# Block sums for adaLN, a two-product group norm, and a fixed four-engine order for the convolution stage

## The chip, the cores and the metric

One core of a Trainium2 chip runs the kernel. The metric is device time in microseconds (us) of one execution. "Before" is the kernel as it stood, "after" the changed one. PE is TensorE, DVE is VectorE, ACT is ScalarE, POOL is GpSimd, and SP is the engine whose queue issues most DMAs.

## The reference

A trunk of two layers runs over 512 tokens of width 1024. Layer 0 mixes tokens with a short gated convolution, layer 1 with a Mamba-2 state-space mixer (SSD). A SwiGLU FFN follows each. Around every sub-layer stand RMS norms and adaLN: the vector c gives a shift, a scale and a gate for each sub-layer.

```
mod = (silu(c) @ ada_w + ada_b).reshape(bsz, DEPTH, 2, 3, D_MODEL)
h = rmsnorm(x, norm_g[i, 0]) * (1.0 + scale) + shift
b_gate, c_gate, v = split(h @ w_in, 3);  y = (b_gate * causal_conv(c_gate * v, conv_w)) @ w_out      # layer 0
y = ssd(...) * silu(z);  y = rms_normalize(y in 8 groups of 256) * norm_g;  y = y @ w_out            # layer 1
x = x + gate * rmsnorm(y, norm_g[i, 1])
y = (silu(gate) * up) @ w_out with gate, up = split(h @ w_in, 2)                                     # FFN
```

All of it is float32.

## The kernel before

**Matmuls.** A weight and its operand are each split into a high part (rounded to fp32r) and a low remainder; three fp32r products (high x high, high x low, low x high: `mm3`, L261 to L264) replace one float32 product. One chunk (`in_chunk`) makes 128 output columns for all 512 tokens with 8 x 3 matmuls. `load_w` (L205) brings two chunks of weights (1 MB) by one DMA on SP into a staging tile `wst`, of which there are two; ACT casts the high part (L202) and DVE subtracts for the low part (L203), into one of four `whl` tiles. `load_wo` (L226) does the same for output matrices, and `load_lead` (L240) for the first weights of the next sub-layer, which go into tiles of their own.

**adaLN.** `ada_set` (L130) handles 512 columns of `ada_w`: four DMAs of 512 KB, and eight multiply-adds on DVE (L124, L126) into `ada_acc`, so that each partition holds the partial sum of its own rows. `ada_finish` (L115) sums over the partitions: four PE transposes of 128x128, then a reduce on DVE (L120). `ada_fin` adds the bias and makes scales and gate columns. There are 20 such sets behind the opening: `ada_next` starts six in the convolution stage and 14 in the first FFN, and finishes each set one call later. `put_gates` turns gate columns into rows and writes them to memory; `make_gg` reads them back as a broadcast tile.

**Convolution stage.** An opening in an order written out by hand (`OPENING`) makes h and the first six chunks (`li`, b, c and v of channels 0 and 1). Then the loop over `jp` makes c and v chunks for two channel blocks, gates them (c copied by ACT, v times c on DVE, the middle tap on ACT, two taps on DVE, then b times that on DVE, high part on ACT, low part on DVE), and six more adaLN sets run beside it. This loop is not in a hand order: a scheduler places each engine's instructions by priority and its own costs. The output product follows in `out_begin` and `out_finish`: half 0 of the columns (`pieces(0)`: k 0 to 3, then 4 and 5), the second half (`pieces(1)`: k 0 to 3), and the rest of k in the boundary, whose order (`BOUNDARY`) is written out: it squares, norms, updates x, transposes, and begins the next sub-layer's six lead chunks. The lead weights of the FFN are loaded in `finish`, behind all loads of the output matrix.

**SSD stage.** Eight groups run in a hand order on PE, ACT and DVE. For each, ACT squares two tiles, DVE adds them (`accg`, L1133), and one float32 matmul with a matrix of ones (`ssg`, L1144) sums over partitions; the root and the scaling follow in the next group's step.

Of the kernel before, what the change touches and what calls it, by code (L numbers as in the profile page):

```python
# [35 lines left out]
def trunk_kernel(  # L36
# [33 lines left out]
    pool.memset(ones, 1.0)  # L70
    mask = consts.tile([P, P], F32, name="mask")
# [7 lines left out]
    csil = consts.tile([P, KD], F32, name="csil")  # L79
# [14 lines left out]
    def other_vectors(stage):  # L94
        d_rows = stage[:16, 3, :].rearrange("p (a b) -> p a b", b=HD)
        d16 = stage[:16, 4, 0:2]
        dma_s(stage[0:16, 0, :], m_norm_g.rearrange("i (r p) -> (i r) p", p=P))
        dma_s(stage[:32, 1, :], m_conv_b.rearrange("i (r p) -> (i r) p", p=P))
        dma_s(stage[:, 2, :], m_conv_w.rearrange("i k (r p) -> (i k r) p", p=P))
        dma_s(d16, m_d.rearrange("i (r p) -> (i r) p", p=2))  # L100
        turned(stage[:, 0, :], mng, 16)
        turned(stage[:, 1, :], mcb, 32)
        turned(stage[:, 2, :], cols3, P)
        dve.tensor_copy(d_rows, d16.unsqueeze(2).to_broadcast([16, 2, HD]))
        turned(d_rows.rearrange("p a b -> p (a b)"), dcol, 16)

# [7 lines left out]

    def ada_finish(acc, ncol, dst):  # L115
        n = ncol // P
        pt = aux_ps("ada_ps")
        for b in range(n):
            pe.transpose(pt[:, b * P:(b + 1) * P], acc[:, b * P:(b + 1) * P], ident)
        dve.tensor_reduce(dst, pt[:, :ncol].rearrange("p (a b) -> p a b", b=P), axis=AX.X, op=ADD)  # L120
# [18 lines left out]
    def ada_fin(col0, acc):  # L139
        q = col0 // P  # L140
        ada_finish(acc, 512, mods[:, q:q + 4])
        dve.tensor_add(mods[:, q:q + 4], mods[:, q:q + 4], adab[:, q:q + 4])
        s, r = divmod(q, 24)
        kind, j = divmod(r, 8)
        if kind == 1:
            dve.scalar_tensor_tensor(acol[:, s * 8 + j:s * 8 + j + 4], mods[:, q:q + 4], 1.0,
                                     ncol(s, 0, j, 4), ADD, MUL)
        elif kind == 2:
            dve.tensor_mul(gcol[:, s * 8 + j:s * 8 + j + 4], mods[:, q:q + 4], ncol(s, 1, j, 4))
# [143 lines left out]
    def put_gates(s):  # L293

        pt = aux_ps("ggp")
        pe.transpose(pt[:KD, :P], gcol[:, s * KD:(s + 1) * KD], ident)
        gr = tmp.tile([KD, P], F32, tag="gr", name="gr", bufs=1)
        dve.tensor_copy(gr, pt[:KD, :P])
        dma(gate_d[s], gr)

# [250 lines left out]
    ada_open = []  # L551

    def ada_next(n):
        for _ in range(max(n, 1)):
            if ada_open:
                ada_fin(*ada_open.pop())
            if ada_sets and n:
                c0 = ada_sets.pop(0)
                ada_open.append((c0, ada_set(c0)))
# [4 lines left out]
    with ExitStack() as ph:  # L564
        ada_p.append(ph.enter_context(tc.tile_pool(name="adap", bufs=3, reuse_waits="tile")))
        actp = ph.enter_context(tc.tile_pool(name="actp", bufs=22, reuse_waits="tile"))
        gx = ph.enter_context(tc.tile_pool(name="gx", bufs=1, reuse_waits="tile"))

# [87 lines left out]
        def busy(dst, n):  # L656

            for _ in range(n):
                pe.matmul(dst, ident, ident, start=True, stop=True)

        with tc.manual_schedule(engines={PE_ENGINE, mybir.EngineType.SP, mybir.EngineType.Activation,
# [121 lines left out]

            for name in OPENING.split():
                step(name)
            later = []
            next_cv = [load_w([(w_in0, (i + 1) * D + 2 * P, 256)], later=later) for i in range(2)]
            for hi, lo in later:
                hi()
                lo()  # L790


        def conv_mix_cv(jc, psc, psv):
            cs = t2("c_sb")
            act.copy(cs, psc)
            cv = t2("cv")
            dve.tensor_mul(cv, psv, cs)
            u = t2("u_cv")
            act.activation(u, cv, AF.Copy, scale=acw[:, 16 + jc:17 + jc])
            dve.scalar_tensor_tensor(u[:, 1:], cv[:, :T - 1], acw[:, 8 + jc:9 + jc], u[:, 1:], MUL, ADD)  # L800
            dve.scalar_tensor_tensor(u[:, 2:], cv[:, :T - 2], acw[:, jc:jc + 1], u[:, 2:], MUL, ADD)
            return u

        def conv_mix_b(u, psb, a):
            dve.tensor_mul(u, psb, u)
            act.copy(a[:, 0, :], u)
            dve.tensor_tensor(a[:, 1, :], u, a[:, 0, :].bitcast(F32), SUB)

        acts = []
        for jp in range(0, KD, 2):  # L810
            if jp == 0:
                pss = lead_ps[:4]
            else:
                ws = next_cv[0] + next_cv[1] if jp == 2 else [
                    w for i in range(2) for w in load_w([(w_in0, (i + 1) * D + jp * P, 256)])]
                pss = [in_chunk(w, h) for w in ws]
            us = [conv_mix_cv(jp + b, pss[b], pss[2 + b]) for b in range(2)]
            wb = load_w([(w_in0, jp * P, 256)]) if jp else None
            for b in range(2):
                a = act_tile(f"bu{jp + b}")  # L820
                conv_mix_b(us[b], in_chunk(wb[b], h) if jp else lead_ps[4 + b], a)
                acts.append(a)
            ada_next(2 if jp < 6 else 0)
            if jp == 4:
                put_gates(0)
                gg = make_gg(0, gg_tile)
                other_vectors(actp.tile([P, 8, P], F32, tag="a", name="rows2"))
        def ffn_lead(i, tile4):
            w1 = f_w_in[i]
            return lambda: [w for c0 in (0, DFF, 256) for w in load_lead([(w1, c0, 256)], tile4)]  # L830

        def ffn_after(i):
            return lambda: load_w([(f_w_in[i], DFF + 256, 256)])

        begun = out_finish(out_begin(0, w_out0, lambda k: acts[k], KD, [gg], xn_tile, "aux",
                                     ffn_lead(0, tile4), ffn_after(0)))


        def ffn(s, i, begun, act_tile, gg_tile, xn_tile, ada, gates, lead, after):
# [13 lines left out]
            for f in range(0, NF, 2):  # L853
# [12 lines left out]
                if f == 18:  # L866
                    for q in gates:
                        put_gates(q)
                    gg = make_gg(s, gg_tile)
# [12 lines left out]
        assert not ada_sets and not ada_open  # L882


    with ExitStack() as ph:
# [99 lines left out]
        class Group:  # L985
# [120 lines left out]
            def step_c(self, q):  # L1106
# [20 lines left out]
                if q == 0:  # L1127
                    self.accg = t2("accg")
                    act.activation(self.accg, y0, AF.Square)
                else:  # L1130
                    sqg = t2("sqg")
                    act.activation(sqg, y0, AF.Square)
                    dve.tensor_add(self.accg, self.accg, sqg)  # L1133
                ygs.append(y0)

            def step_d(self):
                self.sums()
                self.root()
                self.norm()

            def sums(self):

                self.ssg = aux_ps("ssg")
                pe.matmul(self.ssg, ones, self.accg, start=True, stop=True)  # L1144
# [37 lines left out]
        with tc.manual_schedule(engines={PE_ENGINE, mybir.EngineType.Activation, mybir.EngineType.DVE}):  # L1182
# [69 lines left out]
            next(conv2[2])  # L1252
            next(conv2[3])
# [7 lines left out]
            for g in range(1, NG - 1):  # L1261
# [41 lines left out]
                next(conv2[3])  # L1303
                nxt.project_z(0)
# [83 lines left out]
```

## Time and profile before

| | us |
|---|---|
| time, median of 3 runs (lowest, highest) | 1380.81 (1379.1, 1381.97) |
| the profiled execution's own time | 1383.75 |
| its span, first to last instruction | 1382.0 |
| PE busy | 1366.8 |
| DVE busy | 841.6 |
| ACT busy | 535.4 |
| POOL busy | 1.5 |
| mean granted clock of PE | 0.998 of full speed |

Lines of the profile read: line of the code, engine, operation, what it writes <- what it reads, shapes, count | busy time, mean ns of one | idle time of the engine just before, and what ended it. In a timeline the first two figures are start and duration. In a row of windows stand the window, its length, the busy time of PE, PEld (weight loads, beside PE), DVE, ACT and POOL with counts, then PE's granted clock, the DMA engines' busy share and GB/s. A float32 matmul leaves two records.

### The profile page before, as it was taken

Reading aid. Unit: us, or ns where it says so; the run is one execution under the profiler, and the core shown is the slowest. Engines: PE = TensorE matmul, PEld = TensorE weight load, DVE = VectorE, ACT = ScalarE, POOL = GpSimd, SP = SyncE. Lnnn points to the kernel's source line nnn. Section 1 sums busy time; section 2 is a strip of 40 time slices with the busy share of each in tenths; the row PEclk is TensorE's granted clock in tenths of the full one; section 3 lists DMA queues with packets and bytes.
Section 4 is the critical chain, followed back from the end, with each engine's and each line's share of the span. In section 5 each row is a group of like instructions: output and inputs, shape, how many; then the busy total and the mean of one; then the engine's idle time right before and its main releaser. Section 6 shows DMA issues by size and latency. Waiting matters only on the chain.

```text
span 1382.0 us, 17400 instructions
## 1 busy us (share of the span) xinstructions
PE 1366.8 (99%) x7035; PEld 1147.2 (83%) x7035; DVE 841.6 (61%) x1331; ACT 535.4 (39%) x817; POOL 1.5 (0%) x11
## 2 busy tenths in 40 slices
PE   8999999999999999999999999999999999999998
PEld 7788879888888888898888888888888888888886
DVE  5887756487775222759988898897573333332224
ACT  5432256222222211745555445564472322222112
POOL 0000000000000000000000000000000000000000
PEclk9999999999999999999999999999999999999999
DMA  9966661368773223415343423313403223322221
GB/s 313 328 205 230 211 211 62 122 213 268 237 257 122 92 92 102 116 47 172 107 138 109 136 84 115 128 57 121 154 30 107 92 93 113 99 92 92 92 92 62
DMA packets 154181, 190.36 MB, mean 138 GB/s; under 512 B 5860, under 2 KB 111220, under 8 KB 153076
## 3 DMA queue, kind: packets, MB, share of 16 engines
q1 hardware_dynamic: 149952, 176.34, 39.8%
q10 hardware_dynamic: 4148, 12.90, 2.9%
q8 instruction: 55, 0.90, 0.3%
q14 instruction: 26, 0.21, 0.1%
HBM read 186.98 MB, written 2.24 MB: 137 GB/s over the span
## 4 chain that ended last, share of the span: by engine, by line
PE 65%; DMA 1%; DVE 1%; ACT 1%; issue 0%; DVEq 0%; ACTq 0%
PE ip L262 11%; PE ip L264 11%; PE ip L263 11%; PE y L362 7%; PE y L364 7%; PE y L363 7%; PE li L262 2%; PE li L264 2%; PE li L263 2%; PE yd L1118 1%; DMA wst<-in_f_w_in_dram 1%; PE yo L1112 1%; PE xtr L478 1%; PE cb L1057 1%; PE xtok L1040 1%; PE st L1073 0%
## 5 line engine op out<-in xcount | busy, mean ns | idle before, releaser
L262 PE MATMUL ip<-h,whl 128*128 128x512 f32 x1096 | 433.2, 395 | 0.0
L264 PE MATMUL ip<-h,whl 128*128 128x512 f32 x1096 | 427.2, 390 | 0.0
L263 PE MATMUL ip<-h,whl 128*128 128x512 f32 x1096 | 426.8, 389 | 0.0
L262 PEld LDWEIGHTS ip<-h,whl 128*128 128x128 f32 x1096 | 205.8, 188 | 44.1 <-issue 2.6
L263 PEld LDWEIGHTS ip<-h,whl 128*128 128x128 f32 x1096 | 205.9, 188 | 43.2 <-issue 1.4
L264 PEld LDWEIGHTS ip<-h,whl 128*128 128x128 f32 x1096 | 205.7, 188 | 43.3
L203 DVE TENSOR_TENSOR whl<-wst,whl 128x1024 fp32r<-128x1024 f32 (+1 forms) x127 | 133.5, 1070 | 105.9 <-ACT whl L202 105.7
L202 ACT CAST whl<-wst 128x1024 fp32r<-128x1024 f32 (+1 forms) x127 | 114.8, 926 | 202.6 <-PE ip L264 117.1
L203 DVE TENSOR_TENSOR whlo<-wsto,whlo 128x1024 fp32r<-128x1024 f32 x68 | 83.0, 1224 | 176.4 <-ACT whlo L202 176.2
L202 ACT CAST whlo<-wsto 128x1024 fp32r<-128x1024 f32 x68 | 71.2, 1051 | 197.5 <-PE y L364 158.8
L362 PE MATMUL y<-whlo,ff 128*128 128x512 f32 x352 | 137.0, 389 | 0.0
L364 PE MATMUL y<-whlo,ff 128*128 128x512 f32 x352 | 136.9, 389 | 0.0
L363 PE MATMUL y<-whlo,ff 128*128 128x512 f32 x352 | 136.9, 389 | 0.0
L126 DVE SCALAR_TENSOR_TENSOR ada_acc<-ada_st,csil,ada_acc 128x512 f32<-128x512 f32 x140 | 104.9, 749 | 20.0 <-DMA ada_st<-in_ada_w_dram 17.1
L262 PE MATMUL li<-h,whl 128*128 128x256 f32 x288 | 83.4, 290 | 0.0
L847 DVE TENSOR_TENSOR g<-ip,g 128x512 f32<-128x512 f32 x40 | 27.6, 690 | 90.2 <-PE ip L264 90.2
L264 PE MATMUL li<-h,whl 128*128 128x256 f32 x288 | 81.5, 283 | 0.0
L263 PE MATMUL li<-h,whl 128*128 128x256 f32 x288 | 81.5, 283 | 0.0
L846 ACT ACTIVATE g<-ip 128x512 f32<-128x512 f32 x36 | 21.5, 598 | 144.7 <-PE ip L264 144.7
L363 PEld LDWEIGHTS y<-whlo,ff 128*128 128x128 f32 x352 | 66.1, 188 | 13.8
L362 PEld LDWEIGHTS y<-whlo,ff 128*128 128x128 f32 x352 | 66.1, 188 | 13.7
L364 PEld LDWEIGHTS y<-whlo,ff 128*128 128x128 f32 x352 | 66.1, 188 | 13.6
(215 smaller groups left out, 1688.9 us busy)
## 6 DMA issues: line engine op xcount, KB each, us to landing
ada_st<-in_ada_w_dram SPq DMA_DIRECT2D x96, 512.0 KB, 5.7
wst<-in_f_w_in_dram SPq DMA_DIRECT2D x44, 1024.0 KB, 5.2
wsto<-in_f_w_out_dram SPq DMA_DIRECT2D x20, 1024.0 KB, 5.1
wst<-in_m_w_in_dram SPq DMA_DIRECT2D x14, 1024.0 KB, 5.3
wst<-in_m_w_in_dram SPq DMA_DIRECT2D x20, 512.0 KB, 4.2
wst<-in_a_w_in_dram SPq DMA_DIRECT2D x9, 1024.0 KB, 7.1
csb<-cs_d ACTq DMA_DIRECT2D x8, 1024.0 KB, 7.2
wsto<-in_m_w_out_dram SPq DMA_DIRECT2D x7, 1024.0 KB, 5.0
```

The lines of the kernel that those rows point to most:

```text
L126: dve.scalar_tensor_tensor(acc, w, csil[:, k:k + 1], acc, MUL, ADD)
L202: act.copy(dst[:, 0, :nk, :], src)
L203: dve.tensor_tensor(dst[:, 1, :nk, :], src, dst[:, 0, :nk, :].bitcast(F32), SUB)
L262: pe.matmul(dst, w_at(w, 0, kk), a[:, 0, sl], start=start, stop=False)
L263: pe.matmul(dst, w_at(w, 0, kk), a[:, 1, sl], start=False, stop=False)
L264: pe.matmul(dst, w_at(w, 1, kk), a[:, 0, sl], start=False, stop=stop)
L362: pe.matmul(pst, a[:, 0, tk], wt[:, 0, kk, :], start=k == 0, stop=False)
L363: pe.matmul(pst, a[:, 0, tk], wt[:, 1, kk, :], start=False, stop=False)
L364: pe.matmul(pst, a[:, 1, tk], wt[:, 0, kk, :], start=False, stop=k == K - 1)
L478: pe.transpose(pt[:, j * 256 + t * P:j * 256 + (t + 1) * P], self.xn[2 * hi + t][p // 2][:, c:c + P], ident)
L846: act.activation(g, psg, AF.Silu)
L847: dve.tensor_mul(g, psu, g)
```

## The change

- **adaLN.** A set's `ada_acc` is no longer transposed on PE. DVE sums it over blocks of 32 columns with a transpose in the reduce (`ada_fold`), to 16 columns; two sets share one tile `part`, and one float32 matmul with a 0/1 matrix `four` sums the four blocks of partitions for both. `four` is made by five POOL operations at the start. Four small adds place the result.
- **Group norm.** For groups 0 to 6 POOL adds the squares, ACT and DVE split the sum into high and low (`split_sq`), and two fp32r matmuls with `ones_r` replace the float32 one. `ones_r` is made by ACT at the start. Group 7 is as before.
- **Convolution stage.** The loop becomes one sequence of 18 chunks inside the hand order of PE, SP, ACT and DVE. Chunk k's step issues loads, the chunk, the gates of the chunk before, the split of chunk k + 2's weights, low halves, and two to four adaLN multiply-adds. The first loads of the output matrix come at chunk 14. The FFN's three lead loads with their splits (`lead0`) stand ahead of the output matrix's second half.
- Gates 1 to 3 are put out at f = 20 of the first FFN instead of 18, and the turning of the other vectors moves into it (f = 4).

```diff
+    ones_r = consts.tile([P, P], F32R, name="ones_r")
+    act.copy(ones_r, ones)
...
-        for b in range(n):
-            pe.transpose(pt[:, b * P:(b + 1) * P], acc[:, b * P:(b + 1) * P], ident)
-        dve.tensor_reduce(dst, pt[:, :ncol].rearrange("p (a b) -> p a b", b=P), axis=AX.X, op=ADD)
...
+    def ada_fold(acc, dst):
+        dve.tensor_reduce(dst, acc.rearrange("p (b r) -> p b r", r=32), axis=AX.X, op=ADD, apply_transpose=True)
+
+    def ada_fin(col0, part, bank=aux_ps):
...
+        pt = bank("ada_ps")
+        pe.matmul(pt[:, :32], four, part, start=True, stop=True)
+        yield
+        for b in range(4):
+            r = slice(b * 32, (b + 1) * 32)
+            dve.tensor_tensor(mods[r, q:q + KD], pt[r, :32].rearrange("p (q b) -> p q b", b=4)[:, :, b],
+                              adab[r, q:q + KD], ADD)
...
+        four = gx.tile([P, P], F32, tag="four", name="four", bufs=1)
+        pool.tensor_tensor(four[:, 0:64], ident[:, 0:64], ident[:, 64:128], ADD)
...
+            def load_pair(p):
+                jp, kind = 2 + p // 3 * 2, (1, 2, 0)[p % 3]
+                ws.extend(load_w([(w_in0, kind * D + jp * P, 256)], later=splits))
...
+            for k in range(18):
+                i, jp = k % 6, 2 + k // 6 * 2
+                if k % 2 == 0 and k < 14:
+                    load_pair(k // 2 + 2)
+                elif k == 14:
+                    ops = next(parts[0])
+                    splits += [(op,) for op in ops]
+                tiles.append(in_chunk(ws[k], h))
+                if i == 0 and k:
+                    lows.append(gate_b(jp - 1, tiles[k - 1]))
+                elif i in (1, 2):
+                    gate_c(jp + i - 1, tiles[k - 1])
+                elif i in (3, 4):
+                    gate_v(jp + i - 3, tiles[k - 1])
+                    taps(jp + i - 3)
+                elif i == 5:
+                    lows.append(gate_b(jp, tiles[k - 1]))
+                split(k + 2)
+                for low in lows:
+                    low()
+                lows = []
+                for _ in range((3, 4, 3, 2, 2, 2)[i]):
+                    next(madds)
...
+            gate_b(KD - 1, tiles[17])()
+            for op in ops[2:]:
+                op()
+            next(parts[0])
+            next(fins[2])
+            ops = next(parts[0])
+            for op in ops:
+                op()
+            next(fins[2])
+            lead0 = ffn_lead(0, tile4)()
+            begun = out_finish(parts)
...
-                    dve.tensor_add(self.accg, self.accg, sqg)
+                    if g < NG - 1:
+                        pool.tensor_tensor(self.accg, self.accg, sqg, ADD)
+                    else:
+                        dve.tensor_add(self.accg, self.accg, sqg)
...
+            def split_sq(self):
+                self.sqs = ysp.tile([P, 2, T], F32R, tag="ys", name="sqs")
+                hi, lo = self.sqs[:, 0, :], self.sqs[:, 1, :]
+                act.copy(hi, self.accg)
+                dve.tensor_tensor(lo, self.accg, hi.bitcast(F32), SUB)
...
+                if self.g == NG - 1:
+                    pe.matmul(self.ssg, ones, self.accg, start=True, stop=True)
+                else:
+                    for i in range(2):
+                        pe.matmul(self.ssg, ones_r, self.sqs[:, i, :], start=i == 0, stop=i == 1)
```

More of the change, by code (lines that the diff above doesn't have):

```diff
@@ L549, in trunk_kernel @@
         ada_sets += [q0 * P, q0 * P + 512]
-    ada_open = []
+    ada_open, ada_done, small_p = [], [], []
     def ada_next(n):
[L554 to L559, printed above, removed]
+        while ada_done:
+            list(ada_fin(*ada_done.pop()))
+        for _ in range(n if ada_sets else 0):
+            c0 = ada_sets.pop(0)
+            if not ada_open:
+                ada_open.append((c0, small_p[0].tile([P, 32], F32, tag="fold", name="fold", bufs=2)))
+            i = (c0 - ada_open[0][0]) // 512
+            ada_fold(ada_set(c0), ada_open[0][1][:, i * 16:(i + 1) * 16])
+            if i:
+                ada_done.append(ada_open.pop())
     w_in0, w_out0 = a_w_in[0], a_w_out[0]
@@ L828, in ffn_lead @@
[L828 to L836, printed above, removed]
+            for p in range(2):
+                load_pair(p)
+            for _ in range(3):
+                ada_load()
@@ L865, in ffn @@
                 ada(f)
-                if f == 18:
+                if f == 4 and s == 1:
+                    next(vectors)
+                if f == 20:
                     for q in gates:
-                        put_gates(q)
+                        list(put_gates(q))
                     gg = make_gg(s, gg_tile)
@@ L880, in trunk_kernel @@
         h, lead_ps, rest, wz1 = begun
-        assert not ada_sets and not ada_open
+        assert not ada_sets and not ada_open and not ada_done
     with ExitStack() as ph:
```

154 lines of the change are left out of this document (100 added, 54 removed).

## The prediction

> **What bounds the kernel now.** I read the page first, then the waits of TensorE (PE), then busy time by window, then the timelines of the places that the change touches.
>
> ```profile
> PE 1366.8 (99%) x7035; PEld 1147.2 (83%) x7035; DVE 841.6 (61%) x1331; ACT 535.4 (39%) x817; POOL 1.5 (0%) x11
> ```
>
> ```profile
> PE xtr L478 <- ACT xn L469: 3.9, 4, 2.5
> ```
>
> ```profile
> 60.00:163.00 103.00, 103.00 (x467) 84.58 (x466) 82.70 (x124) 31.78 (x41) 0.00 (x0) 1.00 0.70 233
> ```
>
> PE is busy 99% of the span, and the longest wait of PE in the whole trace is 3.9 us at the boundary transposes. In the convolution stage (60 to 163 us) PE never pauses: the figure after the window's length is PE's busy time, and it is the same. So a new order of that stage cannot make PE's work there shorter. It can only take PE instructions away, end a wait elsewhere, or bring in a new wait. DVE is the next engine, with 82.7 of 103 us busy there. (The chain of waits begins only at 441 us in this trace, so for the first third I argue from windows and timelines.) A measurement of this kernel can tell about 0.2%, 2.8 us, from no change.
>
> **adaLN sums on PE.** Each set of 512 columns now ends in four transposes. First the timeline of PE, then the group with its count.
>
> ```profile
> 61.02 0.60 PE L119 MATMUL ada_ps<-ident,ada_acc 128*128 128x128 f32 x4
> ...
> 61.69 0.39 PE L263 MATMUL ip<-h,whl 128*128 128x512 f32 x1
> ```
>
> ```profile
> L119 PE MATMUL ada_ps<-ident,ada_acc 128*128 128x128 f32 x80 | 10.8, 272 | 0.0
> ```
>
> From 61.02 to 61.69 stand four transposes and one 512-column matmul. Such a matmul takes 0.23 (chain below), so a set costs 0.44, and 80/4 = 20 sets cost 8.8 us. After the change DVE folds each set, and one f32 matmul with 32 columns serves two sets: 10 of them. Its price is not in the trace. The nearest rows are the f32 matmuls of the mask stage, in the chain:
>
> ```profile
> 636.82 0.89 PE cb L1057 x8
> ...
> 746.25 0.86 PE ssg L1144 x2
> 747.11 0.23 PE ip L262
> ```
>
> Four f32 matmuls of 128 columns (two records each) take 0.89, so 0.22 each; by columns alone a quarter of that, 0.05. I take 0.2, since the 128 weight columns are the same: 2.0 us, ends 0.5 and 2.2. **Gain 6.8 us.** The Trainium skill ("TensorE: Matmul & The Clock Gate", Back-to-back issue gap) gives about 25 ns for up to 64 columns; by that, as an estimate, ten pairs of passes cost 0.5 and the total would come out 1.5 us lower. No row here shows a 32-column f32 matmul.
>
> **Group norm.** One f32 product of 512 columns takes 0.86, two fp32r products 2 x 0.23. Seven of eight groups change: 7 x 0.40 = **2.8 us gained**, if their operand is ready.
>
> ```profile
> 738.51 0.69 DVE L1133 TENSOR_TENSOR accg<-accg,sqg 128x512 f32<-128x512 f32 x1 [0.70 <-ACT sqg L1132]
> ```
>
> The squares are there at 738.5, and PE asks at 746.25 (chain above). In between go the add on POOL (unseen; at least the 0.69 of DVE, and 4 us would still fit), ACT's high half (0.62) and DVE's low half (0.68) behind three taps and two splits. On ACT and DVE the work is one instruction more and none more; I cost it at nothing. The cover gone, every us is on PE seven times.
>
> **First boundary.** The two pauses of PE there:
>
> ```profile
> 205.07 0.39 PE L364 MATMUL y<-whlo,bu 128*128 128x512 f32 x1
> 206.29 0.33 PE L478 MATMUL xtr<-ident,xn 128*128 128x128 f32 x1 [0.84 <-ACT xn L469]
> 206.91 0.55 PE L478 MATMUL xtr<-ident,xn 128*128 128x128 f32 x3 [0.28 <-ACT xn L469]
> ```
>
> The starts are 1.22 apart where 0.23 would do, and 0.62 where 0.11 would: 1.5 us. The reason stands on ACT, with the loads on SP and DVE's share:
>
> ```profile
> 176.59 11.82 SPq L245 DMA_DIRECT2D wst<-in_f_w_in_dram  x3
> ```
>
> ```profile
> 183.62 2.18 ACT L202 CAST whl<-wst 128x512 fp32r<-128x512 f32 x4 [2.87 <-DMA wst<-in_f_w_in_dram]
> ...
> 195.64 2.18 ACT L202 CAST whl<-wst 128x512 fp32r<-128x512 f32 x4 [1.48 <-DMA wst<-in_f_w_in_dram]
> ```
>
> ```profile
> 184.28 2.50 DVE L203 TENSOR_TENSOR whl<-wst,whl 128x512 fp32r<-128x512 f32 x4 [2.27 <-ACT whl L202]
> ```
>
> The FFN's lead weights are split on ACT and DVE ahead of the boundary's first square; the third load lands at 195.6, so ACT comes to the square only at 197.8. With these splits earlier the 1.5 us go. **Gain 1.5.** What is late next is what the three loads now stand in front of.
>
> **The new wait.** In the fixed order SP issues: half 0 of w_out (two loads), the three lead loads, then the second half of w_out, all through the two `wst` buffers. Each load waits until the load two before it has been split. Call E the end of the last chunk on PE. The second w_out load is split only behind the last gate product (DVE), its copy and its high half (ACT). When does DVE get there? Its durations in the stage, and ACT's:
>
> ```profile
> L126 DVE SCALAR_TENSOR_TENSOR ada_acc<-ada_st,csil,ada_acc 128x512 f32<-128x512 f32 x43 | 32.1, 748 | 6.5 <-DMA ada_st<-in_ada_w_dram 5.7
> L203 DVE TENSOR_TENSOR whl<-wst,whl 128x1024 fp32r<-128x1024 f32 x14 | 17.1, 1218 | 0.7 <-ACT whl L202 0.7
> ...
> L807 DVE TENSOR_TENSOR bu<-u_cv,bu 128x512 fp32r<-128x512 f32 x7 | 4.8, 682 | 0.0
> ...
> L120 DVE TENSOR_REDUCE mods<-ada_ps 128x4 f32<-128x512 f32 x5 | 3.2, 680 | 0.0
> L124 DVE TENSOR_SCALAR ada_acc<-ada_st,csil 128x512 f32<-128x512 f32 x5 | 2.4, 478 | 0.0
> ```
>
> ```profile
> L202 ACT CAST whl<-wst 128x1024 fp32r<-128x1024 f32 x14 | 14.8, 1054 | 36.3 <-PE ip L264 36.3
> L799 ACT ACTIVATE u_cv<-cv,cols 128x512 f32<-128x512 f32 x8 | 5.8, 723 | 6.8 <-DVE cv L797 6.8
> L806 ACT CAST bu<-u_cv 128x512 fp32r<-128x512 f32 x7 | 4.3, 619 | 2.3 <-DVE u_cv L805 2.3
> ```
>
> ```profile
> 166.37 3.90 DVE L126 SCALAR_TENSOR_TENSOR ada_acc<-ada_st,csil,ada_acc 128x512 f32<-128x512 f32 x5
> ...
> 198.77 1.28 DVE L415 TENSOR_TENSOR yg<-y,gg 128x512 f32<-128x512 f32 x2
> ```
>
> The five multiply-adds that need each other start 0.79 apart; two that don't overlap by 0.08. DVE's fixed list up to the end of the last chunk's step is: 20 splits x 1.22 = 24.4; 42 multiply-adds x 0.79 and 6 first ones x 0.5 = 36.2; 22 products and low halves x 0.68 = 15.0; 16 taps, of the multiply-adds' kind, x 0.75 = 12.0; 6 block sums at the reduce's 0.68 = 4.1 (unseen; 0.3 to 1.4); small ones 1.9. Sum 93.6, less 70 x 0.08 = 5.6. Then come waits that the fixed order puts into DVE: seven times the taps stand behind ACT's 0.72 (5.6), six times a split stands behind gate copy and high half, 0.62 + 1.05 (10.2). Together 103.8, begun 1.9 after the first lead accumulator is done (copy, high half): 105.7. PE from the same moment: 3.4 for the other five accumulators, 0.4 until DVE has freed the first bank, 18 x 24 x 0.2267 = 97.9 (the matmuls' spacing: 432 in the stage), 0.4 for the small ones: E = 102.1. DVE is 3.6 behind. The splits of the weights have 10.9 us of lead, so PE doesn't feel that inside the stage. After it: product 0.68, copy 0.62, halves 1.05 and 1.22 make 3.7, so the second w_out load is split at E + 7.3. From there the loads, by the two tiles' landing times in this stretch (first `wst`, then `wsto`):
>
> ```profile
> DMA to landing us min/median/max: 5.1/6.3/7.6
> ```
>
> ```profile
> DMA to landing us min/median/max: 3.7/4.6/5.5
> ```
>
> Second lead load 5.5 (two in flight, nothing of adaLN beside them), its split 3.2 (183.62 to 186.78 above), w_out's second half 4.6, first split 2.3: ready at E + 22.9. PE wants it after 72 matmuls and a small one: E + 16.5. **PE stands 6.4 us.** And the clock, by windows around the only like gap:
>
> ```profile
> 1004.00:1007.50 3.50, 1.03 (x5) 0.44 (x3) 3.23 (x9) 3.44 (x12) 0.00 (x0) 1.00 0.20 69
> 1007.50:1011.00 3.50, 3.22 (x12) 2.50 (x12) 1.11 (x2) 3.29 (x9) 0.00 (x0) 0.63 0.00 0
> ```
>
> ```profile
> 1007.23 0.33 PE L478 MATMUL xtr<-ident,xn 128*128 128x128 f32 x1 [2.47 <-ACT xn L469]
> ```
>
> After 2.47 us in which PE stood idle (the bracket) the granted clock is 0.63 over the next 3.5 us: matmuls at half speed for 3.4 us, **1.7 us lost**. I charge that here too. The Trainium skill ("TensorE: Matmul & The Clock Gate", What's actually happening) says half rate follows a full idle window of about 3.4 us, so a shorter gap may escape; this trace's did not.
>
> **Opening.** The new copy on ACT may bring a table load ahead of the first rows, and five POOL operations stand before the zeroing of a row. The price lies between nothing and one table load, and ACT stands idle 0.24 us ahead of its first root:
>
> ```profile
> L1148 ACT ACT_TABLE_LOAD x8 | 10.3, 1283 | 6.6 <-PE ssg L1144 4.5 <-issue 2.0
> ```
>
> ```profile
> 5.90 0.29 ACT L633 ACTIVATE ss<-ss,eps 128x1 f32<-128x1 f32 x1 [0.24 <-DVE xn L622]
> ```
>
> I take 0.3 (0 to 1.3).
>
> **Sum**, against the profiled execution (span 1382.0, 1383.75 with what lies around it): -6.8 - 2.8 - 1.5 + 0.4 + 0.3 + 6.4 + 1.7 = -2.3, so 1381.4 there. That execution is 2.9 above the median shown; from the median, 1380.8 - 2.3 = **1378.5 us**. Gates and vectors that move within the FFN keep their PE instructions and have tens of us to spare: nothing.
>
> **Rivals.** Without the stand and the clock the sum is -10.4. (a) DVE keeps pace, and the last gate runs at E. The split is then at E + 3.7 and PE stands 2.8 us: 2.8 more, -7.6, or -5.9 with the clock lost: 1373 to 1375. For it: DVE is busy only 83 of 103 us today. Against: today's order lets it fill its waits, the fixed one does not. (b) Slower: DVE falls further behind. Each us of lag is a us of PE's stand. Net zero is at a stand of 8.7 us, slower by 0.2% from 11.5, a split at E + 12.4. Block sums that transpose and add in two goes (1.36, +4.1) and a lead load of 7.6 (+2.1) give a stand of 12.6: +3.9, 1384.7. For it: 16 us of waits inside DVE's order. Against: no row shows a two-go reduce. (c) The change doesn't do what it says: w_out's second half gets its buffer ahead of the lead loads. Then only -10.4 stays: 1370.4. Against: SP is in the fixed order too.
>
> **Chances.** Forecast 0.48 (stand 4.5 to 8.5, matmul price 0.5 to 2.2: 1375 to 1381), (a) 0.24, (b) 0.20, (c) 0.08. Faster by over 0.2% (under 1378.0): (a), (c) and 0.42 of the forecast's own, 0.52; within: 0.28; slower: 0.20. The range leaves out most of (c), and half of (b): 1371.5 to 1384.5.
>
> **What would show it.** Right: a wait of PE at L362 for `whlo` splits of 5 to 8 us some 16 us after the last chunk, granted clock under 1 behind it, no wait for ACT at the first transposes, `ssg` in two records of 0.23, ten `ada_ps` matmuls of about 0.2 in place of 80 records. Wrong: no such wait (the buffers or the order are not as I read them), gaps of PE between chunks (DVE is the bound inside the stage), or a pause ahead of `ssg` in the SSD groups (POOL is too slow).

## The result and the profile after

The changed kernel takes 1385.7 us (median of 5 runs, 1384.53 to 1386.15); the kernel before took 1380.61 on the same chip (1379.1 to 1381.97). The ratio is 1.0031, with a 95% interval of 1.0019 to 1.0044: slower, by about 5 us, where 2.3 us of gain were forecast. The profiled execution took 1384.91 us, with a span of 1383.1. Its first lines on the page and the waits of PE (line waited for <- what ended the wait: us in total, times, longest):

```profile
PE 1359.4 (98%) x6975; PEld 1143.5 (83%) x6975; DVE 846.2 (61%) x1344; ACT 540.7 (39%) x827; POOL 11.6 (1%) x23
```

```profile
PE y L373 <- ACT whlo L211: 6.8, 1, 6.8
PE ptr L93 <- DVE mods L150: 4.9, 1, 4.9
...
PE y L374 <- DVE whlo L212: 0.5, 1, 0.5
...
PE ip L271 <- DVE cv L862: 0.2, 1, 0.2
```

PE is busy 7.4 us less than before, and yet the end comes later: two waits that the kernel before did not have. The first is the one that was forecast, at the second half of `w_out`. The second, for a PSUM bank ahead of a turned vector (`ptr`) in the first FFN, nobody had forecast. The wait for `xn` at the boundary transposes (3.9 us before) is gone.

**The forecast stand.** PE's timeline, and windows around it (columns as before: PE's busy time first, the granted clock after the five engines):

```profile
176.21 0.39 PE L375 MATMUL y<-whlo,bu 128*128 128x512 f32 x1
183.44 0.80 PE L373 MATMUL y<-whlo,bu 128*128 128x512 f32 x1 [6.84 <-ACT whlo L211]
184.70 0.80 PE L374 MATMUL y<-whlo,bu 128*128 128x512 f32 x1 [0.46 <-DVE whlo L212]
185.29 0.63 PE L375 MATMUL y<-whlo,bu 128*128 128x512 f32 x1
185.72 0.63 PE L373 MATMUL y<-whlo,bu 128*128 128x512 f32 x1
...
188.71 0.47 PE L374 MATMUL y<-whlo,bu 128*128 128x512 f32 x1
189.01 0.39 PE L375 MATMUL y<-whlo,bu 128*128 128x512 f32 x1
```

```profile
183.00:187.00 4.00, 3.09 (x6) 2.13 (x7) 2.36 (x2) 1.68 (x3) 0.00 (x0) 0.50 0.46 139
187.00:191.00 4.00, 4.00 (x15) 3.23 (x14) 1.23 (x1) 0.77 (x2) 0.00 (x0) 0.77 0.87 302
```

Between 176.21 and 183.44 nothing starts. Then the starts are 0.43 apart, not 0.23, up to 188.71, and the clock's column says 0.50.

**The other one.** PE and DVE in the first FFN, and the window behind the wait:

```profile
286.49 0.39 PE L271 MATMUL ip<-h,whl 128*128 128x512 f32 x1
291.83 0.25 PE L93 MATMUL ptr<-ident,rows 16*128 16x16 f32 x1 [4.95 <-DVE mods L150]
292.01 0.80 PE L272 MATMUL ip<-h,whl 128*128 128x512 f32 x1
```

```profile
285.26 0.74 DVE L123 SCALAR_TENSOR_TENSOR ada_acc<-ada_st,csil,ada_acc 128x512 f32<-128x512 f32 x1
288.95 1.54 DVE L123 SCALAR_TENSOR_TENSOR ada_acc<-ada_st,csil,ada_acc 128x512 f32<-128x512 f32 x2 [2.94 <-DMA ada_st<-in_ada_w_dram]
...
291.00 0.68 DVE L150 TENSOR_TENSOR mods<-ada_ps,cols 32x8 f32<-32x8 f32 x4
291.71 0.17 DVE L94 COPY cols<-ptr 128x16 f32<-128x16 f32 x1
```

```profile
292.00:296.00 4.00, 4.00 (x10) 3.14 (x10) 4.00 (x10) 0.00 (x0) 0.00 (x0) 0.50 0.51 154
```

The fourth turned vector needs one of four small PSUM banks. One is held by adaLN's product `ada_ps` until DVE has made the four adds of L150. On DVE these stand behind multiply-adds, and DVE idles 2.94 us there for a load of `ada_w`. So PE, in its order, stands for a DMA that it has nothing to do with, and then for the DVE work that had piled up behind that DMA. (The fourth vector's own operand was long there: DVE had made it at 108.0.) Ten 512-column matmuls in 4.00 us follow, half the pace.

**Where the time went, by stage.** Each stage runs from the first start of one matmul group to that of the next in PE's timeline. "Before again" is a second profile of the unchanged kernel, taken with the experiments (1378.99 us, span 1377.2).

| stage, us | before | before again | after |
|---|---|---|---|
| opening, to the first chunk `ip` | 61.38 | 61.53 | 61.13 |
| 18 chunks, to the first `y` | 101.62 | 101.60 | 98.72 |
| half 0, to half 1's first matmul | 16.45 | 16.46 | 23.59 |
| half 1, to the last `y` of this stage | 29.00 | 28.61 | 30.55 |
| first FFN's lead and first steps | 37.82 | 37.82 | 37.80 |
| first FFN's chunks | 213.96 | 213.87 | 217.58 |
| first FFN's output product | 119.92 | 119.92 | 120.04 |
| boundary and SSD's lead | 29.27 | 29.27 | 29.24 |
| SSD groups | 300.35 | 300.35 | 297.62 |
| SSD's output and boundary | 100.44 | 96.75 | 95.98 |

Two readings that a total hides. The SSD boundary of the first profile of before held 3.7 us that "before again" doesn't have: there is no wait for `xn` at this boundary now, and what is left, 0.7 us in two waits, is at the first boundary.

```profile
PE xtr L478 <- ACT xn L469: 0.7, 2, 0.5
```

So that wait of 2.5 us comes and goes from execution to execution (what brings it, no run shows), and the stage that holds it makes 3.7 of the 4.8 us by which the two profiled executions of before differ. And the changed kernel gives up 7.1 us at half 1, 1.9 behind it and 3.7 in the first FFN, against 2.9 gained in the chunks and 2.7 in the SSD groups.

**What each new operation took.** The group of the small product, one of them in PE's timeline, the two products of the group norm and the add on POOL (in grouped lines: minimum, median, maximum in ns, first and last start):

```profile
L146 PE MATMUL ada_ps<-fold,four x20: 190/232/273, 104.7 to 447.1; 128*128 128x32 f32 x20
```

```profile
104.75 0.30 PE L146 MATMUL ada_ps<-fold,four 128*128 128x32 f32 x2
104.89 0.48 PE L271 MATMUL ip<-h,whl 128*128 128x512 f32 x1
105.20 0.40 PE L272 MATMUL ip<-h,whl 128*128 128x512 f32 x1
```

```profile
L1266 PE MATMUL ssg<-sqs,ones_r x14: 389/389/389, 673.7 to 916.1; 128*128 128x512 f32 x14
```

```profile
L1247 POOL TENSOR_TENSOR accg<-accg,sqg x7: 1293/1297/1303, 668.6 to 908.4; 128x512 f32<-128x512 f32 x7
```

From 104.75 to 105.20 stand one product (two records) and one 512-column matmul of 0.23: a product costs 0.22 us.

### The profile page after: what moved, and what is told of

It reads as the page before. It is cut to its first block, busy times and chain, and to the rows that moved or that the text cites. A ratio compares the mean times of both kernels' runs of the same rounds, so it can differ in the third digit from the quotient of the medians.

```text
span 1383.1 us, 17303 instructions
## 1 busy us (share of the span) xinstructions
PE 1359.4 (98%) x6975; PEld 1143.5 (83%) x6975; DVE 846.2 (61%) x1344; ACT 540.7 (39%) x827; POOL 11.6 (1%) x23
## 4 chain that ended last, share of the span: by engine, by line
PE 84%; DVE 8%; DMA 4%; ACT 2%; SPq 2%; issue 1%; ACTq 0%; DVEq 0%
PE ip L271 15%; PE ip L272 15%; PE ip L273 15%; PE y L374 9%; PE y L373 9%; PE y L375 9%; DVE ada_acc L123 3%; DMA ada_st<-in_ada_w_dram 3%; PE li L271 2%; PE li L273 2%; PE li L272 2%; PE li L763 1%; DVE whl L230 1%; PE yd L1231 1%; SPq L621 1%
## 5 line engine op out<-in xcount | busy, mean ns | idle before, releaser
L271 PE MATMUL ip<-h,whl 128*128 128x512 f32 x1096 | 431.5, 394 | 0.2 <-DVE cv L862 0.2
L271 PEld LDWEIGHTS ip<-h,whl 128*128 128x128 f32 x1096 | 206.6, 188 | 44.1 <-issue 1.8
L212 DVE TENSOR_TENSOR whl<-wst,whl 128x1024 fp32r<-128x1024 f32 (+1 forms) x113 | 116.5, 1051 | 106.3 <-ACT whl L211 106.0
L211 ACT CAST whl<-wst 128x1024 fp32r<-128x1024 f32 (+1 forms) x113 | 100.2, 910 | 142.6 <-PE ip L273 64.0
L123 DVE SCALAR_TENSOR_TENSOR ada_acc<-ada_st,csil,ada_acc 128x512 f32<-128x512 f32 x140 | 104.3, 748 | 19.2 <-DMA ada_st<-in_ada_w_dram 16.4
L230 DVE TENSOR_TENSOR whl<-wst,whl 128x1024 fp32r<-128x1024 f32 x60 | 72.6, 1218 | 20.4 <-ACT whl L229 20.4
L271 PE MATMUL li<-h,whl 128*128 128x256 f32 x288 | 83.2, 289 | 0.0
```

The lines of the kernel that those rows point to most:

```text
L123: dve.scalar_tensor_tensor(acc, w, csil[:, k:k + 1], acc, MUL, ADD)
L211: act.copy(dst[:, 0, :nk, :], src)
L212: dve.tensor_tensor(dst[:, 1, :nk, :], src, dst[:, 0, :nk, :].bitcast(F32), SUB)
L230: lambda sw=sw, w=w: dve.tensor_tensor(w[:, 1, :nk, :], sw, w[:, 0, :nk, :].bitcast(F32), SUB)))
L271: pe.matmul(dst, w_at(w, 0, kk), a[:, 0, sl], start=start, stop=False)
```

## The experiments

Theory A, from the two traces: the two waits are separate mistakes of place, each with a half-clock period behind it, and everything else about the change is a gain. The rival: DVE is now too late in general, and a wait that is mended comes back elsewhere.

| kernel | time, us | ratio to before, 95% interval |
|---|---|---|
| e1, lead loads last | 1376.23 | 0.9973 (0.9962 to 0.9984) |
| e2, vectors at f = 2 | 1381.66 | 1.0008 (0.9998 to 1.0017) |
| e3, half the multiply-adds | 1384.76 | one run |
| e4, before again | 1378.99 | one run |
| e5, e1 and e2 together | 1371.59 | 0.9941 (0.9928 to 0.9955) |
| e6, e3 with late adds | 1377.03 | one run |
| e7, late adds alone | 1384.09 | one run |
| e9, vectors in the chunks | 1380.39 | 1.0002 (0.9993 to 1.001) |
| e10, block sums alone | 1383.41 (1379.13 to 1387.87) | 1.0013 (0.9998 to 1.0028) |
| e11, PE kept busy in the stand | 1382.11 | one run |
| e12, vectors in the chunks, copy early | 1372.39 | 0.994 (0.992 to 0.996) |
| e13, e12 with sets spread | 1370.05 | 0.992 (0.9904 to 0.9936) |

Beside these runs the kernel before took between 1378.65 and 1386.17 us, so a kernel of a single run is judged by the stages of its trace and not by its time.

**e1: the lead loads behind all loads of `w_out`, as before.**

```diff
-            parts = out_begin(..., lambda: lead0, ffn_after(0))
+            parts = out_begin(..., ffn_lead(0, tile4), ffn_after(0))
...
-            lead0 = ffn_lead(0, tile4)()
```

> The changed kernel with the FFN's three lead loads put back behind all loads of the output matrix (in finish), all else as changed. Theory A (the stand of 7.0 us at the output matrix's second half comes from the lead loads ahead of it in the two staging buffers): the stand and the half clock behind it (some 3 us) go, the first boundary's pause of about 1.5 us comes back: about 8.5 us off, 1377 us. Rival B (VectorE reaches the last gate too late, whatever stands ahead on the queue): a stand of several us stays, 1382 to 1386 us.

Measured: 1376.23, with the stand gone (half 0 takes 16.59 us again) and the boundary's pause back. The waits of PE in this kernel:

```profile
PE ptr L93 <- DVE mods L150: 5.9, 1, 5.9
...
PE xtr L489 <- ACT xn L480: 1.1, 2, 0.8
```

The two spans lie 9.1 us apart (1383.1 and 1374.0); 0.6 of it is in the opening, ahead of anything that was changed here, so the lead loads' place cost 8.5 us. The wait that moving them was to end was worth 1.1; the one they made, 7.1 and the clock.

**e2: the other vectors turned at f = 2.**

```diff
-                if f == 4 and s == 1:
+                if f == 2 and s == 1:
                     next(vectors)
```

> The changed kernel with the turning of the other vectors one step of the FFN earlier (f = 2 instead of 4), where no adaLN finish stands beside it. Theory A (the fourth transpose waits for a PSUM bank that an adaLN finish holds until VectorE, waiting for a load, has read it): the pause of 5.1 us and the half clock of some 3 us behind it go, 1377.5 us. Rival B (it waits for the rows or for VectorE as such): the pause moves along, 1385 us.

Measured: 1381.66. The first FFN's chunks take 212.92 us in place of 217.58: 4.7 gained where 8 were expected. The bank wait is gone, so its own Rival B fell (the pause did not move along with the vectors). But a part of the time comes back, as the rival at the head of this section has it, where PE waits for a weight split:

```profile
PE ip L273 <- DVE whl L212: 2.0, 3, 1.0
```

These waits are short, and the granted clock stays at 1.00 in each 10 us of the stage.

**e3: every second multiply-add of the six sets in the convolution stage left out** (half of those sums is missing), to bring DVE on time.

```diff
-                        ada_madd(acc, st[:, k, :], kh * 2 + k)
+                        if k == 0:
+                            ada_madd(acc, st[:, k, :], kh * 2 + k)
```

> The changed kernel with every second multiply-add of the convolution stage's six adaLN sets left out (half of those sums is missing), so 24 VectorE instructions fewer, some 19 us of its time; all loads and the order as changed. Theory A (the stand is the lag of VectorE plus the chain of two loads and two splits): the last gate runs at the last chunk's end, and the stand falls from 7.0 to about 3 us. Rival B (the loads alone set it): it stays at 7 us.

Measured: 1384.76, and the stand is still 6.7 us. DVE's timeline says why:

```profile
162.05 1.23 DVE L212 TENSOR_TENSOR whlo<-wsto,whlo 128x1024 fp32r<-128x1024 f32 x1 [0.27 <-ACT whlo L211]
170.72 0.69 DVE L150 TENSOR_TENSOR mods<-ada_ps,cols 32x8 f32<-32x8 f32 x4 [7.45 <-PE ada_ps L146]
171.45 0.17 DVE L155 SCALAR_TENSOR_TENSOR acol<-mods,cols 128x8 f32<-128x8 f32 x1
171.53 4.90 DVE L212 TENSOR_TENSOR whl<-wst,whl 128x512 fp32r<-128x512 f32 x8
```

The chunks ended at 159.50 here, and DVE splits the second load of `w_out` at 162.05, 2.6 us behind them. Then it idles 7.45 us in front of four small adds. They wait for the third pair's product on PE, which is queued behind the 48 matmuls of `w_out`'s k 0 to 3 (10.9 us). The lead splits stand behind these adds in DVE's order, and the second half's load behind the lead splits. That DVE's lag makes the stand, as the prediction has it, is thus not the whole: without the lag another wait, which the prediction didn't name, ends at the same place.

**e6 and e7: those adds behind the lead splits, with half the multiply-adds (e6; half of those sums missing) and with all (e7).**

```diff
-            next(fins[2])
             lead0 = ffn_lead(0, tile4)()
+            next(fins[2])
```

> Every second multiply-add of the six adaLN sets of the convolution stage left out (half of those sums is missing), and DVE's adds that finish the third pair of sets put behind the splits of the lead loads. Theory A (with DVE on time, the stand is set by these adds: they wait for a PE product that is queued behind half 0's first 48 matmuls, and the lead splits stand behind them): lead splits begin some 5 us earlier, PE stands 1.5 to 3.5 us in place of 6.8 and keeps its clock, and the time is 1376 to 1379. Rival B (the chain of loads through the two staging tiles sets the stand, whatever DVE does): 6 to 7 us as before, 1384.

> The changed kernel with all its multiply-adds, and only DVE's adds that finish the third pair of sets put behind the splits of the lead loads. Theory A (DVE's lag and the wait for the third pair end almost together, so taking one away shows the other): the stand is 5.5 to 7 us, the time 1383 to 1386. Rival (the adds alone make the stand): the stand falls to 4 us or less, and the time to 1379 or less.

Measured: 1377.03 and 1384.09. In e6 PE's stand is down to this:

```profile
177.59 0.49 PE L373 MATMUL y<-whlo,bu 128*128 128x512 f32 x1 [1.65 <-ACT whlo L211]
178.85 0.50 PE L374 MATMUL y<-whlo,bu 128*128 128x512 f32 x1 [0.76 <-DVE whlo L212]
```

In e7 it is as in the changed kernel:

```profile
PE y L373 <- ACT whlo L211: 6.7, 1, 6.7
```

So either cause alone is enough for the stand, and only both together taken away end it. In the changed kernel they end within a few us of each other, which its DVE and SP show:

```profile
165.40 0.65 DVE L875 TENSOR_TENSOR u_cv<-ip,u_cv 128x512 f32<-128x512 f32 x1
...
167.70 1.23 DVE L212 TENSOR_TENSOR whlo<-wsto,whlo 128x1024 fp32r<-128x1024 f32 x1 [0.26 <-ACT whlo L211]
171.07 0.69 DVE L150 TENSOR_TENSOR mods<-ada_ps,cols 32x8 f32<-32x8 f32 x4 [2.15 <-PE ada_ps L146]
...
174.68 2.50 DVE L212 TENSOR_TENSOR whl<-wst,whl 128x512 fp32r<-128x512 f32 x4 [0.31 <-ACT whl L211]
```

```profile
168.95 5.82 SPq L254 DMA_DIRECT2D wst<-in_f_w_in_dram  x2
177.21 8.97 SPq L238 DMA_DIRECT2D wsto<-in_a_w_out_dram  x3
```

E is 159.85. The split at 167.70 frees a buffer and lets the second lead load go at 168.95; that load's split ends at 177.18, and only then SP can issue `w_out`'s second half at 177.21, when PE has already asked for it for 0.8 us.

**e11: PE kept busy in the stand.** 28 matmuls more, on a bank that half 1 overwrites.

```diff
                     ys[hf] = [mk[hf](f"y{hf}{t}") for t in range(4)]
+                    if (s, hf) == (0, 1):
+                        for _ in range(28):
+                            pe.matmul(ys[hf][0][:, :P], ident, ident, start=True, stop=True)
```

> The changed kernel with 28 matmuls of 128x128 more, on a bank that half 1 then overwrites, put between half 0 and half 1 of the output product, so that PE works through most of its stand. Theory A (behind the stand the clock is halved and costs 2.5 to 3 us of PE's time): the stand's length stays, all matmuls behind it stand 0.23 apart, and the time is 2 to 3 us under the changed kernel's: 1382.5 to 1383.5. Rival (the clock costs the 1.7 of the prediction, or nothing): 1384 to 1385.7.

Measured: 1382.11, with a span of 1380.3. The stand's length is the same (23.53 us from E to half 1's first matmul), and behind it PE keeps its pace:

```profile
182.00:186.00 4.00, 2.71 (x12) 1.87 (x11) 2.39 (x3) 1.63 (x3) 0.00 (x0) 1.00 0.41 131
```

Half 1 takes 28.61 us in place of 30.55: the clock behind the stand costs 1.9 us. The rest of the 2.8 us between the two spans lies elsewhere (0.7 ahead of E, 0.2 in the first FFN). So the total came out where Theory A has it, and yet its size for the clock was too high: it counted the whole 5.3 us at half pace, and the first of those matmuls wait for DVE's low half at any clock (0.76 us in this kernel, 0.46 in the changed one).

**e9: the lead loads last, and the vectors turned in the convolution stage.**

```diff
+                if k == 11:
+                    next(vectors)
```

> The lead loads behind all loads of the output matrix, and the four turned vectors put back into the convolution stage, at chunk 11, behind loads that were issued five chunks earlier. Theory A (the turned vectors cost nothing but their place: what costs is the wait for a PSUM bank that a block sum of adaLN holds): no wait of PE for adaLN's adds in the first FFN, and FFN chunks of 209.5 us in place of 217.6; the time is 8 us under the 1376.2 of the lead loads moved alone, about 1368, 0.991 of before. Rival (the queue of adaLN loads in the first FFN makes PE stand once, whatever is turned there): the pause comes back at a weight split, as when the vectors moved to f = 2, and the time is 1372.

Measured: 1380.39, a miss by 12 us for Theory A and by 8 for its rival. The first FFN is as its rival said (212.19 us, with waits for weight splits), and the convolution stage lost 8.8 us:

```profile
126.71 0.56 PE L93 MATMUL ptr<-ident,rows 16*128 16x16 f32 x3
132.93 0.28 PE L93 MATMUL ptr<-ident,rows 16*128 16x16 f32 x1 [5.65 <-DVE rows L107]
```

The fourth vector is first spread out by a DVE copy (L107). Written into the same step, that copy stands in DVE's order, 6 us behind PE's. PE falls back onto DVE's clock once, and pays the half clock besides.

**e12: the same, with that copy two chunks earlier. e13: e12 with the first FFN's sets spread evenly.**

```diff
-                if k == 11:
+                if k in (9, 11):
                     next(vectors)
...
-                    lambda f: ada_next((1, 1, 2, 2, 2, 1, 2, 1, 2, 0, 0)[f // 2]), (1, 2, 3),
+                    lambda f: ada_next((1, 1, 2, 1, 2, 1, 2, 1, 2, 1, 0)[f // 2]), (1, 2, 3),
```

(In e12 a `yield` parts the copy from the turning.)

> As the kernel with lead loads last and the vectors turned in the convolution stage, but the DVE copy that the fourth turned vector needs stands two chunks ahead of the turning. Theory A (PE stood there 5.7 us for DVE's place in the order, and for nothing else): PE's stand in the stage is under 0.5 us, the convolution chunks take 98.8 to 99.5 us, the first FFN's 212.2 as in that kernel, and the time is 1380.4 less 8.8, about 1371.5, and between 1370 and 1372. Rival (a PSUM bank held by a product that DVE reads late makes the turned vectors wait in any case): a stand of 2 to 5 us, and 1375 to 1379.

> The kernel of the run before it, with the 14 sets of adaLN in the first FFN spread 1 1 2 1 2 1 2 1 2 1 0 over its steps in place of 1 1 2 2 2 1 2 1 2 0 0. Theory A (the waits for weight splits left in the first FFN come from two sets in each of three steps in a row, which keep DVE behind): they fall from 2.2 us to under 1, with the half-clock behind them, and the time is 2 to 3 us lower, about 1369. Rival (any step with two sets makes such a wait): no change.

Measured: 1372.39 and 1370.05. In e12 the four turned vectors go through without a pause:

```profile
126.86 0.73 PE L93 MATMUL ptr<-ident,rows 16*128 16x16 f32 x4
```

and the chunks take 99.60 us. In e13 the waits for weight splits are gone and the first FFN's chunks take 210.66 in place of 212.81; a new wait for the gates has come at its end:

```profile
PE ggp L306 <- DVE gcol L158: 1.6, 1, 1.6
```

**e5: e1 and e2 together.**

> Both repairs at once: the lead loads back behind all loads of the output matrix, and the other vectors turned at f = 2 instead of f = 4. Theory A (the two stands are separate, each with its own half-clock period): the stand at w_out's second half and the one at the turned vectors are both gone, the 1.5 us at the first boundary are back, and the time is that with the lead loads moved alone, 1376.2, less the 4.0 that moving the vectors alone gained: about 1372, 0.994 of before. Rival (the gain of one is taken up by the other, because DVE and the queue of loads are the common limit): no better than 1376.

Measured: 1371.59, where the two gains add up as Theory A said. e1, e5, e12 and e13 beat both kernels, with intervals wholly under 1; e13 is the best of this study, 0.992 of before. The rival at the head of this section holds for a small part: with the vectors moved, e2, e5, e9 and e12 show waits of 1.6 to 2.9 us for weight splits that the changed kernel doesn't have.

**e10: the kernel before with the block sums alone** (`ada_fold`, `ada_fin`, `four`, as in the change).

> The kernel before with the block sums of adaLN alone (ada_fold, one product for two sets, four); no fixed order in the convolution stage, lead loads and turned vectors where they were. By the prediction's term, with the small product at its measured 0.15 us: 8.8 - 1.5 = 7.3 us gained, 2.9 of it in the convolution chunks and 5 in the first FFN: about 1373. Rival (DVE's place in the first FFN has no slack, and the four adds and a transposing reduce in its order make PE wait there for weight splits): the 2.9 stay, the first FFN gains 2 or less, and the time is 1376 to 1377.

Measured: 1383.41 (1379.13 to 1387.87), ratio 1.0013. Neither expectation held for the time; the first FFN's chunks took 209.09 us, 4.8 less than before, as the term said, and the gain was lost in the convolution stage, in its profile at 131 us:

```profile
136.12 0.28 PE L91 MATMUL ptr<-ident,rows 16*128 16x16 f32 x1 [4.63 <-DMA rows<-in_m_norm_g_dram]
```

There the scheduler placed PE's turning of the vectors ahead of the moment when ACT's queue issues their loads. The turned vectors again, and again with the clock at 0.50 behind it. The profiled execution was the fastest of its runs; what made the others longer by up to 8.7 us no trace here shows.

**e4: the kernel before once more.**

> The kernel before, unchanged, for a second profile. Theory A (the 4.5 us that the changed kernel's profile is shorter at the second boundary are a matter of how fast the lead loads landed in that execution): the pause of 2.5 us before the transposes of that boundary is smaller or gone here. Rival B (the change removed it): it is there again, 2.5 us.

Measured: 1378.99, with the stages of the table above. Theory A held: the 2.5 us are not there.

## Why the prediction was wrong

It forecast 2.3 us of gain and the traces show 5.9 of loss (1377.2 to 1383.1, with "before again" as the one that has no chance wait). Term by term:

| term | predicted | measured | from |
|---|---|---|---|
| adaLN's sums on PE | -6.8 | -7.0 | first FFN in e10 -4.8; chunks -2.2 (6 x 0.44 less 2 x 0.22) |
| group norm | -2.8 | -2.7 | SSD groups |
| stand at half 1 | +6.4 | +7.1 | half 0's stage, e1 |
| clock behind it | +1.7 | +1.9 | e11 |
| first boundary | -1.5 | -1.1 | `xtr` waits of e1 |
| first chunk's bank | +0.4 | +0.2 | wait of `ip` L271 |
| opening | +0.3 | -0.4 | its stage (-0.4 to -1.1 in all profiles with the new opening) |
| gates and vectors that move | nothing | +7.8 | below |

The terms add up to 5.8, but not stage for stage: half 1 shows nothing of the first boundary's gain, and the SSD boundary, which has no term, is 0.8 us shorter than in "before again".

The step that failed is the last sentence of the sum: "Gates and vectors that move within the FFN keep their PE instructions and have tens of us to spare: nothing." The vectors don't move within the FFN: the kernel before turns them in the convolution stage (first one at 131.73, last at 135.56 us), the changed one in the first FFN. The instructions do keep their price: the chunks lose some 0.7 us of turned vectors, and the first FFN gains as much. But the first FFN's chunks take 217.58 us where e10, with the same sums and no turned vectors, takes 209.09. Of these 8.5, 5.0 are the wait at 291.83, 0.8 the four transposes, and the rest the half clock. Less the 0.7 that left the convolution stage, the move costs 7.8 in this trace. Not all of that comes back when the vectors are taken out: in e9 these chunks take 212.19 us, 5.4 less than in the changed kernel but 3.1 more than in e10, with 2.2 us of waits for weight splits. e10's first FFN is also the easier one: between 252 and 470 us, 29 loads of `ada_w` are issued in it, 49 in the changed kernel and in e9. That the long stand hides the split waits in the changed kernel is likely and not shown.

The prediction counted slack in the vectors' own need (they are used in the SSD stage, 300 us later) and didn't ask what else the transposes need: a PSUM bank, whose holder is freed by DVE behind a DMA. With this term put in, its 1378.5 would have been 1386.3; the median is 1385.7. That this comes so near is partly luck, since the other terms miss by up to 0.7 us each and nearly cancel. None of its rivals had this place, and the range ended 1.2 us short. All its signs of being right came: the wait at `w_out`'s second half, the clock under 1 behind it, no wait for ACT at the transposes, the two short `ssg` records, ten small products of about 0.2 us. They stood only at the places it had thought of.

Its other main step, the stand, was right in place, length and clock, though for a reason that was only half of it. The second load of `w_out` is split at E + 9.1 where E + 7.3 was worked out (the last gate product runs 5.55 behind E, not 3.6: from 61.0 to 165.4 us DVE is busy for 85.2 of 104.4, so it idled 19.2 us where 15.8 us of waits were worked out), and the loads and splits behind it take less than charged. But DVE's lag isn't the only thing that holds the lead splits back: rival (a), DVE on time, would by e3 have given 6.7 us of stand and not 2.8, since the adds of the third pair wait for PE behind 48 matmuls. The prediction had named what stands behind the waiting loads on SP, and not what stands ahead of the splits on DVE. Its sum is also off on the way: seven times 0.72 is 5.0 and not 5.6, six times 1.67 is 10.0 and not 10.2, and the four terms behind the last gate make 3.6 and not 3.7. Set right, they give a stand of about 5.4 us, so a part of the nearness of 6.4 to 7.1 is luck. (The 3.9 us that it calls PE's longest wait are four waits together; the longest is 2.5.)

The rest of the cases: (b) named a time, 1384.7, that lies within 1.0 us of the measured one by luck: its stand was 12.6 us, the measured one is 7.1, and the block sum is one instruction of 0.71 us, not two goes. (c) fell: the loads went in the order of the code. The first boundary gained what was said, but in the stage table it doesn't show: half 1 waits about as long for DVE's low half of the late weights (e11, where the clock is full, has half 1 at 28.61, no better than "before again").

Of the clock, the row of before that the prediction leaned on (half rate behind an idle time of 2.47 us) held for longer gaps: those of 4.63 (e10), 4.95 and 6.84 us (after) and 5.65 (e9) were each followed by a window at 0.50. The Trainium skill ("TensorE: Matmul & The Clock Gate", What's actually happening) has the half rate begin after an idle window of about 3.4 us that runs freely. The gaps of 4.6 to 6.8 us agree with it, and so do those of 1.61 (e5) and 1.65 us (e6), which kept the full clock; the 2.47 us of the trace of before do not, and in the stand of 6.84 us the half rate had set in after 2.0 us (last section).

## What to carry to other kernels

A small instruction that is moved keeps its price and takes its needs along: before you call the move free, list what it waits for (a bank, an operand, a DMA's issue on another queue) and which engine, how far behind, sets each of them free. In a fixed order, put what one engine makes for another at least its lag ahead of the use: the same four transposes cost about 8 us in three places (a bank in the FFN, a copy in the same step, a load not yet issued) and under 1 us where the copy stood two chunks earlier. And a load that is brought forward through a small ring of buffers is paid by whatever now stands behind it: here a wait of 1.1 us was traded for 7.1 and a slow clock.

## What the runs showed of the hardware

- **The half clock keeps to a grid of 3.41 us.** It doesn't begin where PE takes up work again, nor last a fixed time behind that. Ahead of the stand PE's last matmul ends at 176.60 and the next starts at 183.44. Two rows of 1 us, in which the granted clock changes:

```profile
178.00:179.00 1.00, 0.00 (x0) 0.00 (x0) 0.00 (x0) 0.00 (x0) 0.00 (x0) 0.81 1.06 326
188.00:189.00 1.00, 1.00 (x4) 0.79 (x3) 0.96 (x1) 0.00 (x0) 0.00 (x0) 0.57 1.03 399
```

A mean of 0.81 is 0.38 us at 0.50, so the half rate sets in at 178.62, 2.0 us into the stand; 0.57 puts its end at 188.86, 10.24 us later. Read in the same way, it lasts 6.8 us at the second wait (from 291.26) and 3.4 us in the trace of before (from 1008.38, with PE at work again since 1007.23). These are three, two and one times 3.41 us, and the two starts in the trace after lie 33 times 3.41 us apart. Cut the traces of this case into such stretches from the first recorded change of the clock (6 to 9 us) to the last, and a half period stands behind every stretch at full rate in which PE, by its records, idled 2.0 us or more, and behind none in which it idled 1.8 us or less.

So where a gap falls counts beside how long it is: in e6 the gaps of 1.65 and 0.76 us fall into two stretches (1.05 and 1.37 us idle), and the granted clock stayed at 1.00; the 2.47 us of before fell into one. The full rate came back behind a stretch with 0.46 us of idle time (e7) and not behind one with 0.58 (after). In e5, too, PE idled 1.61 us ahead of this row, and the clock stayed at 1.00:

```profile
372.40 0.50 PE L273 MATMUL ip<-h,whl 128*128 128x512 f32 x1 [1.61 <-DVE whl L212]
```

- **A narrow float32 product isn't cheap.** 32 columns take 0.22 us in their two passes, as much as 128 columns (0.89 for four).
- **POOL as a helper.** Its add of 128x512 takes 1.30 us, DVE's took 0.69. It stood beside other work in all seven groups, and PE waited for none of them.
